# Unit 1's gate half by seven block products; four sums of h on GpSimd; three transfers made earlier

## The chip, the cores and the metric

The kernel runs on one core of a Trainium2 chip. The core has TensorE (PE; its weight loads are shown apart as PEld), VectorE (DVE), ScalarE (ACT), GpSimd (POOL) and SyncE (SP), each with an instruction queue of its own that it works through in order. Transfers are issued from the queues of SP and POOL. The metric is the device time of one execution in microseconds (us); lower is better.

## The reference

One layer of an encoder on 512 tokens with a model width of 2048, in float32. What matters here:

```python
h = rms_norm(x, pre_mix_g[l])
z = h @ w_in[l]                                  # q, k, v and u
a = chunked_attention(q, k, v, rel_bias[l])      # 8 heads of 128
p = multiscale_pool(u, pool_w[l], pool_scale[l])
m = jnp.concatenate([a, p], axis=-1) @ w_o[l]
x = x + rms_norm(m, post_mix_g[l])
h = rms_norm(x, pre_ffn_g[l])
up = causal_dwconv(h @ w_up[l], conv_w[l], conv_b[l])
y = (jax.nn.gelu(up[..., :D_FF], approximate=True) * up[..., D_FF:]) @ w_down[l]
x = x + rms_norm(y, post_ffn_g[l])
```

D_FF is 5632. The product h @ w_up has 2 x 5632 columns.

## The kernel before

**Numbers.** Every float32 operand is split into a rounded high part and a rest (`split`, lines 138 to 146: ScalarE rounds at L140, VectorE subtracts at L141). A plain product takes three matmuls of 512 columns for each block of 128 x 128 weights (`mm3`, L162, L164, L165). Products by the seven block products of Strassen's scheme take their block factors from sums of quarters of the weights and of h; `mm2` (L170 and L176) does each with one matmul of 512 and one of 256 columns for a block of weights.

**Stages.** The tokens' half products with w_in come first: q and k, then v (`v_steps`), then the other heads of q and k by seven blocks, then the heads' attention and u. Then come the products with w_o (`wo_product`), the norm, and h, turned and split, in four tiles gT0 to gT3 (`hT`). Then w_up: 5632 columns are 22 units of 256, and each unit has a gate half (p = 0) and an up half (p = 1). The first PLAIN = 3 halves (unit 0's two, unit 1's gate half) are plain products. The rest, 41 halves, are done by seven blocks (`Factors`, `seven`, `keep`, `keep_all`). Last come the products with w_down.

**Around the change.** Unit 0's halves go to four PSUM banks, `ups`, of the eight that the pool has. `h_sums(i)` for i = 0, 1 makes the sums of h's quarters that the seven blocks need: h5, h6 and h3 (tiles `hs`), each half (i) in turn. `whole` adds high part and rest of a quarter into one tile of 128x1024 (L1301), four times for each i; subtractions follow (L1309, L1312, L1314, L1317), and splits into `hs`. `h_difference` then overwrites one quarter of h by a difference. `up(1, 0, ...)` is unit 1's plain gate half; between its quarters it calls `spread2`, which turns the norm's factor into rows on TensorE (L223), and copies them out of PSUM as R on VectorE (L1267), and the gate and product of unit 0, which read `ups` and so free its banks.

The blocks of the series are named (k, i): half k, product i of 1, 6, 7, 4 (bank qa), 5, 3 (qg) and 2 (qd). The order is written out: it begins (0,1), (0,2), (0,5), (1,1), (0,3), then goes on by a table of places. Products 1, 7, 2 and 4 read quarters of h itself; 5, 3 and 6 read h5, h3 and h6. Each block's weights, a raw tile of 128x1024, are split ahead (four blocks ahead, `AHEAD`) into one of four pairs of tiles; between two uses GpSimd's queue adds another quarter of w_up to the raw tile by an accumulating transfer (L1365). The raw tiles come over SP's queue (L1348).

**Transfers of sums.** `sums_in_dram` builds sums of blocks of w_o (`wt`) and of w_down (`t`) in device memory, by copies and accumulating transfers; `more_sums(n)` makes the next n of them. While `paced` is set, each is issued from GpSimd's queue behind a small memset that waits for the VectorE split last issued. Afterwards copies go over SP's queue. `ready_blocks` splits three blocks of w_down among the w_o products and writes them back.

**Order.** TensorE's instructions stand as the program writes them. The order on the other engines is set by the framework's scheduler when the program is built, and is fixed in the built program.

Of the kernel before, what the change touches and what calls it, by code (L numbers as in the profile page):

```python
# [27 lines left out]
EPS = 1e-6  # L28
WARM = 9
NU = KF // 2  # L30
PLAIN = 3
CU = 4
AHEAD = 3
SCALE = 1.0 / math.sqrt(DH)
# [47 lines left out]
def encoder_layer(ctx: ExitStack, tc: tile.TileContext, x, xT, vecs, rel, post_mix, post_ffn,  # L82
# [23 lines left out]
    def bank(name):  # L106
        return psum.tile([P, 512], F32, tag="ps", name=name)
# [221 lines left out]
    def more_sums(n):  # L329
        for _ in range(n):  # L330
            next(sums_step, None)
# [166 lines left out]
    psv = [bank(f"v0_{t}") for t in range(NT)]  # L498
    sums_of_x = x_sums()
    for n, _ in enumerate(v_steps(0, psv)):  # L500
        if n in (1, 3, 5, 7, 9, 11, 13):
            more_sums(1)
        for _ in range(2):
            next(sums_of_x, None)
        if n == 9:
            for i, v in enumerate(differences):
                split(*(hT[i][:, :, at, :] for at in AT[1]), v)
            early_x.close()
            p0 = mixing_w.enter_context(tc.tile_pool(name="p0", bufs=1, reuse_waits="tile"))
# [103 lines left out]
    with tc.tile_pool(name="p1", bufs=2, reuse_waits="tile") as p1:  # L613
# [156 lines left out]
        for h in range(3):  # L770
            if not h:
                run(2)
                ready_head(0)
            run(1)
            scores(h)
            if h:
                more_sums(1)
            run(1)
            if h:
                values(h - 1)  # L780
                more_sums(1)
            run(1)
            ready_head(h + 1)
            run(1)
            turn(h)
            if not h:
                v_ready()
# [3 lines left out]
        def mid(h):  # L791
            def step():
                values(h)
                more_sums(2 if h in (3, 4) else 1)
                if h == 2:
                    scores(3)
                elif h + 2 < HEADS:
                    ready_head(h + 2)
                if h == 3:
                    v_load(1)  # L800
            return step
# [37 lines left out]
        def ready_blocks():  # L839
            for at, j in ready_parts:  # L840
                v, hi = (p2.tile([P, 1024], dt, tag=tag, name=tag) for tag, dt in (("rw", F32), ("rwh", F32R)))
                lo = v.bitcast(F32R)
                nc.sync.dma_start(v.rearrange("p (a b) -> p a b", a=2),
                                  first_block(at[0], at[1] - 1, 0)[:, 2 * j:2 * j + 2, :])
                for _ in range(4):
                    yield
                split(hi, lo, v)
                yield
                for dest, part_ in zip(ready_w[at], (hi, lo)):
                    nc.sync.dma_start(dest[:, 2 * j:2 * j + 2, :], f32(part_).rearrange("p (a b) -> p a b", a=2))  # L850
                for _ in range(2):
                    yield

        ready_steps = ready_blocks()

        def wo_product(i, cc, left, between=None):
            ps = [bank(f"m{i}{cc}{t}") for t in range(2)]
            if cc and i in (2, 5, 6, 3):
                more_sums(1)
            for q in range(4):  # L860
                w = weights.get(f"wo{i}_{cc}_{q}")
# [343 lines left out]
    with tc.tile_pool(name="p3", bufs=2, reuse_waits="tile") as p3:  # L1205
# [40 lines left out]
                nc.vector.tensor_mul(z[:, j, :], ps[j], R)  # L1246
            return z

        def up(u, p, between=()):
            ps = [bank(f"up{u}_{p}_{j}") for j in range(2)]  # L1250
            between = list(between)
            for i in range(4):
                w = weights.get(f"w{p}{u}_{i}")
                factors.prefetch(4 - len(weights.specs) + weights.used)
                for kb in range(4 * i, 4 * i + 4):
                    for j in range(2):
                        mm3(ps[j], part(w, j, slice(kb % 4 * P, (kb % 4 + 1) * P)), g_both(hT, kb),
                            kb == 0, kb == KD - 1)
                step = between.pop(0) if between else None
                if step:  # L1260
                    step()
            return ps

        def spread2():
            psr = bank("R2")
            spread(psr, rt)
# [30 lines left out]
        def h_sums(i):  # L1297
            def whole(k, t):
                v = raw_x(f"q{k}{t}").rearrange("p (a b) -> p a b", a=4)
                hi, lo = quarter(k, t, i)  # L1300
                nc.vector.tensor_add(v, f32(hi), f32(lo))  # L1301
                return v

            def keep(n, v):
# [20 lines left out]
        class Factors:  # L1325
# [20 lines left out]
            def load(self, k, i):  # L1346
# [2 lines left out]
                    self.raw[k, what] = tile_  # L1349

                if i == 1 and (k, "w") not in self.raw:
                    raw("w" if k in self.alone else "x", raw4("wx") if k == self.alone[0] else raw_x("wx"), 0, 0)
                elif i == 5 and k == self.alone[0]:
                    raw("x", raw4("wx"), 0, 0)
                    self.add(k, "x", 1, 0)
# [55 lines left out]
        def keep(k, i):  # L1411
# [10 lines left out]
            elif i == 6:  # L1422
                zs[k, "m"] = pair_tile("zm", 2)
                v = wide(zs[k, "m"][:, :1])
                keep.six = nc.scalar.activation(v, banks[k, "a"], AF.Copy).ins  # L1425
                nc.vector.tensor_add(v, banks.pop((k, "g")), v)
            elif i == 7:
                v = wide(zs[k, "m"][:, 1:])
# [26 lines left out]
        def first_left():  # L1455
# [4 lines left out]
            split(hi, lo, v)  # L1460
            return hi, lo

        for i in range(2):
            h_sums(i)
        z = up(1, 0, [spread2, lambda: product(0, gate(0, normed(ups[0])), normed(ups[1]))])
        z = normed(z)
        rights, firsts = [right(0, cc) for cc in range(2)], []
        for r in rights:
            next(r)
# [8 lines left out]
        for k, i in factors.order:  # L1478
            seven(k, i)
            keep(k, i)  # L1480
            if (k, i) == factors.order[0]:
                with ExitStack() as behind:
                    for ins in factors.third:
                        behind.enter_context(tc.issue_after(ins))
                    h_difference()
            if (k, i) == (0, 6):
                with tc.issue_after(keep.six):
                    gates[1] = gate(1, z)
            if (k, i) == (end, 6):
                summed.close()  # L1490
                pr = ctx.enter_context(tc.tile_pool(name="pr", bufs=2, side="right", reuse_waits="tile"))
# [256 lines left out]
```

## Time and profile before

| | us |
|---|---|
| three runs, median (lowest, highest) | 1858.98 (1856.39, 1862.3) |
| the profiled execution's own time | 1859.2 |
| its span, first to last instruction | 1857.4 |
| granted TensorE clock | 0.999 |
| PE busy, of the span | 1843.6 |
| DVE busy | 1540.8 |
| ACT busy | 1082.3 |
| POOL busy | 303.2 |

How to read what follows. A row of a timeline gives the start in us, the length in us, engine, line, operation, output tile <- input tiles, shape, how many instructions the row merges, and in brackets how long the engine was idle before it and what ended that. A matmul's length is that of one, and they overlap, so the start of the next counts. Rows of stretches give the stretch, its length, then busy time and number of instructions on PE, PEld, DVE, ACT and POOL, the granted clock, the busy share of the DMA engines, and GB/s. Rows of waits give who waited, for whom, the total, the number and the longest.

### The profile page before, as it was taken

The page shows a single profiled execution, that of the slowest core. Times are in us where ns is not written, and L with a number is a line of the kernel's source. Part 1 is how long each engine was busy: PE and PEld are TensorE (multiplying, and loading weights), DVE is VectorE, ACT ScalarE, POOL GpSimd, SP SyncE. Part 2 cuts the span into 40 slices and gives each one's busy share as a digit, 9 for nine tenths or more (in the row PEclk, how much of TensorE's full clock was granted, in tenths as well). Part 3 has the DMA queues.
Part 4 walks back from the last instruction along what each step waited for, and adds up shares of the span by engine and source line. Part 5 has one row for each costly group of instructions (what it writes and reads, how often), then busy time and mean ns, then how long its engine had stood idle before and what let it go on. Part 6 is the DMA issues. An engine that isn't in the chain of part 4 may idle for free.

```text
span 1857.4 us, 25457 instructions
## 1 busy us (share of the span) xinstructions
PE 1843.6 (99%) x9598; PEld 1584.8 (85%) x9598; DVE 1540.8 (83%) x1804; ACT 1082.3 (58%) x1376; POOL 303.2 (16%) x402
## 2 busy tenths in 40 slices
PE   9999999999999999999999999999999999999998
PEld 7888888888878888888888888888888888888886
DVE  6988777887698988888888888888887899899876
ACT  7654455456464666566666665656655655565553
POOL 3411000100000122212222122121121001111101
PEclk9999999999999999999999999999999999999999
DMA  8599978999994798988888888899888967777785
GB/s 319 174 318 297 320 232 236 267 255 331 348 328 144 186 213 195 208 210 195 203 198 206 209 199 198 204 206 202 200 176 293 363 220 175 193 210 178 176 229 159
DMA packets 139338, 426.01 MB, mean 229 GB/s; under 512 B 11920, under 2 KB 15376, under 8 KB 133520
## 3 DMA queue, kind: packets, MB, share of 16 engines
q0 software_dynamic: 54864, 173.56, 46.1%
q1 hardware_dynamic: 84352, 250.84, 38.4%
q8 instruction: 75, 1.23, 0.3%
q14 instruction: 47, 0.39, 0.1%
HBM read 370.35 MB, written 104.33 MB: 256 GB/s over the span
## 4 chain that ended last, share of the span: by engine, by line
PE 93%; DMA 3%; DVE 2%; ACT 1%; issue 1%; SPq 0%; DVEq 0%; POOL 0%; POOLq 0%; ACTq 0%
PE qa L170 18%; PE qa L176 10%; PE qg L170 9%; PE qg L176 5%; PE qd L170 4%; PE pa L164 4%; PE pa L165 4%; PE pa L162 4%; PE qd L176 2%; PE pg L164 2%; PE pg L165 2%; PE pg L162 2%; PE m L164 2%; PE m L165 2%; PE m L162 2%; PE v L164 2%
## 5 line engine op out<-in xcount | busy, mean ns | idle before, releaser
L140 ACT ACTIVATE wfh<-wx 128x1024 fp32r<-128x1024 f32 x192 | 203.4, 1059 | 152.7 <-PE qg L170 55.4
L170 PE MATMUL qa<-gT,wfh 128*128 128x512 f32 x1152 | 288.6, 392 | 0.0
L141 DVE TENSOR_TENSOR wfl<-wx,wfh 128x1024 fp32r<-128x1024 f32 x192 | 234.7, 1222 | 59.8 <-ACT wfh L140 44.8
L170 PEld LDWEIGHTS qa<-gT,wfh 128*128 128x128 f32 x1152 | 207.2, 189 | 37.1
L1365 POOL DMA_DIRECT2D wx<-in_w_up x122 | 104.7, 858 | 502.2 <-DVE wfl L141 473.8
L140 ACT ACTIVATE wfh<-wy 128x1024 fp32r<-128x1024 f32 x96 | 101.7, 1060 | 109.3 <-PE qg L170 57.9
L170 PE MATMUL qg<-h,wfh 128*128 128x512 f32 x656 | 162.2, 389 | 0.9 <-ACT zb L1421 0.9
L176 PE MATMUL qa<-gT,wfl 128*128 128x256 f32 x1152 | 161.2, 283 | 0.1
L176 PEld LDWEIGHTS qa<-gT,wfl 128*128 128x128 f32 x1152 | 151.6, 191 | 4.3 <-ACT zm L1425 0.3
L170 PEld LDWEIGHTS qg<-h,wfh 128*128 128x128 f32 x656 | 122.9, 188 | 26.7 <-ACT zb L1421 1.3
L141 DVE TENSOR_TENSOR bl<-b,bh 128x2048 fp32r<-128x2048 f32 x56 | 127.2, 2287 | 19.1 <-ACT bh L140 11.7
L140 ACT ACTIVATE bh<-b 128x2048 fp32r<-128x2048 f32 x56 | 106.1, 1913 | 55.1 <-DVE b L1129 22.8
L141 DVE TENSOR_TENSOR wfl<-wy,wfh 128x1024 fp32r<-128x1024 f32 x96 | 117.2, 1221 | 10.9 <-ACT wfh L140 6.4
L162 PE MATMUL pa<-bh,ah 128*128 128x512 f32 x320 | 124.5, 389 | 0.0
L164 PE MATMUL pa<-bl,ah 128*128 128x512 f32 x320 | 124.5, 389 | 0.0
L165 PE MATMUL pa<-bh,al 128*128 128x512 f32 x320 | 124.5, 389 | 0.0
L141 DVE TENSOR_TENSOR wfl<-wz,wfh 128x1024 fp32r<-128x1024 f32 x48 | 58.7, 1224 | 54.1 <-PE qa L170 54.1
L176 PEld LDWEIGHTS qg<-h,wfl 128*128 128x128 f32 x656 | 89.5, 190 | 6.4
L170 PE MATMUL qd<-gT,wfh 128*128 128x512 f32 x384 | 94.9, 389 | 0.0
L176 PE MATMUL qg<-h,wfl 128*128 128x256 f32 x656 | 91.5, 282 | 0.0
L170 PEld LDWEIGHTS qd<-gT,wfh 128*128 128x128 f32 x384 | 72.0, 188 | 14.9
L170 PE MATMUL qa<-h,wfh 128*128 128x512 f32 x328 | 82.1, 392 | 0.0
(550 smaller groups left out, 4363.5 us busy)
## 6 DMA issues: line engine op xcount, KB each, us to landing
wx<-in_w_up POOLq DMA_DIRECT2D x122, 512.0 KB, 6.1
b<-in_w_down SPq DMA_DIRECT2D x32, 1024.0 KB, 6.8
wt<-in_w_o POOLq DMA_DIRECT2D x24, 1024.0 KB, 15.8
wx<-in_w_up SPq DMA_DIRECT2D x43, 512.0 KB, 5.5
wz<-in_w_up SPq DMA_DIRECT2D x41, 512.0 KB, 6.0
wy<-in_w_up SPq DMA_DIRECT2D x41, 512.0 KB, 4.6
wy<-in_w_up POOLq DMA_DIRECT2D x41, 512.0 KB, 6.9
sum<-part POOLq DMA_DIRECT2D x38, 512.0 KB, 6.8
```

What stands on the lines that cost most here:

```text
L140: rounded = nc.scalar.activation(hi, src, AF.Copy)
L141: rest = nc.vector.tensor_sub(lo, src, f32(hi))
L162: nc.tensor.matmul(ps, l[0], r[0], start=first, stop=False, skip_group_check=onto)
L164: nc.tensor.matmul(low, l[0], r[1], start=False, stop=False, skip_group_check=onto)
L165: nc.tensor.matmul(ps, l[1], r[0], start=False, stop=last, skip_group_check=onto)
L170: nc.tensor.matmul(ps, w[0][:, kb], pairs[kb][0], start=fresh and not kb, stop=last, skip_group_check=not fresh)
L176: nc.tensor.matmul(ps[:, sl], w[1][:, kb], pair[:, sl], start=False, stop=last, skip_group_check=not fresh)
L1365: nc.gpsimd.dma_start(self.raw[k, what], self.block(k, m, kh), accum_op=ALU.add)
```

## The change

PLAIN becomes 2: unit 1's gate half joins the series as its half k = 0, which now has 42 halves. `up` goes away. `factors.prefetch(4)` comes ahead of the sums of h; `spread2` comes behind block (0,1), and the gate and product of unit 0 behind (0,2). Of the eight additions in `whole` the four of i = 0 move to GpSimd. The half k = 1 takes its first raw tile from the five tiles of `raw4`. One transfer of sums more is made among v, one more in the first head and one more in a later step of the heads; three fewer are left among the w_o products. The waits in `ready_blocks` are cut another way at the same total. The gate of unit 1, which stood behind (0,6) with an order of its own, is made by `keep_all`.

```diff
-PLAIN = 3
+PLAIN = 2
...
-        if n in (1, 3, 5, 7, 9, 11, 13):
+        if n % 2:
             more_sums(1)
...
             scores(h)
-            if h:
-                more_sums(1)
+            more_sums(1)
...
-                more_sums(2 if h in (3, 4) else 1)
+                more_sums(2 if h in (3, 4, 5) else 1)
...
-                for _ in range(4):
+                for _ in range(5):
                     yield
                 split(hi, lo, v)
                 yield
                 for dest, part_ in zip(ready_w[at], (hi, lo)):
                     nc.sync.dma_start(dest[:, 2 * j:2 * j + 2, :], f32(part_).rearrange("p (a b) -> p a b", a=2))
-                for _ in range(2):
-                    yield
+                yield
...
-            if cc and i in (2, 5, 6, 3):
+            if cc and i == 5:
                 more_sums(1)
...
-        def up(u, p, between=()):
...
                 hi, lo = quarter(k, t, i)
-                nc.vector.tensor_add(v, f32(hi), f32(lo))
+                (nc.vector if i else nc.gpsimd).tensor_add(v, f32(hi), f32(lo))
...
-                    raw("w" if k in self.alone else "x", raw4("wx") if k == self.alone[0] else raw_x("wx"), 0, 0)
+                    raw("w" if k in self.alone else "x", raw4("wx") if k < 2 else raw_x("wx"), 0, 0)
...
-                keep.six = nc.scalar.activation(v, banks[k, "a"], AF.Copy).ins
+                nc.scalar.activation(v, banks[k, "a"], AF.Copy)
...
+        factors.prefetch(4)
         for i in range(2):
             h_sums(i)
-        z = up(1, 0, [spread2, lambda: product(0, gate(0, normed(ups[0])), normed(ups[1]))])
-        z = normed(z)
...
                     h_difference()
-            if (k, i) == (0, 6):
-                with tc.issue_after(keep.six):
-                    gates[1] = gate(1, z)
+                spread2()
+            if (k, i) == factors.order[1]:
+                product(0, gate(0, normed(ups[0])), normed(ups[1]))
```

The changed program's lines are numbered a little lower: the additions of `whole` are L1284, the subtractions L1292 to L1300, the copy of R is L1250, the accumulating transfer L1348.

**First place: where the sums of h begin.** On GpSimd, before, behind the norm's roots (`small`, `rt`):

```order
L967 TENSOR_TENSOR small<-small,mhalf 128x2 x2
L218 TENSOR_TENSOR rt<-rt,mhalf 128x4
L1365 DMA wx<-in_w_up 128x1024 x3
L1365 DMA wy<-in_w_up 128x1024
L1365 DMA wx<-in_w_up 128x1024
L1236 DMA gd_0_5687<-ca 128x2x256
```

and now (q are the quarters' sums of `whole`, gT the tiles of h):

```order
L965 TENSOR_TENSOR small<-small,mhalf 128x2 x2
L1348 DMA wx<-in_w_up 128x1024
L218 TENSOR_TENSOR rt<-rt,mhalf 128x4
L1284 TENSOR_TENSOR q_5732<-gT_5003 128x1024
L1284 TENSOR_TENSOR q_5734<-gT_5001 128x1024
L1284 TENSOR_TENSOR q_5739<-gT_5001 128x1024
L1284 TENSOR_TENSOR q_5745<-gT_5003 128x1024
L1348 DMA wx<-in_w_up 128x1024 x2
```

The four additions stand behind the root L218, and an accumulating transfer stands ahead of it. On VectorE, before:

```order
L1057 TENSOR_REDUCE small<-small 128x4
L217 TENSOR_SCALAR rt<-small 128x4
L1301 TENSOR_TENSOR q_5716<-gT_4996 128x1024
L1301 TENSOR_TENSOR q_5718<-gT_4994 128x1024
L1301 TENSOR_TENSOR q_5723<-gT_4994 128x1024
L141 TENSOR_TENSOR w_0l<-w_0r,w_0h 128x1024
L1309 TENSOR_TENSOR q_5716<-q_5716,q_5718 128x1024
```

and now:

```order
L1055 TENSOR_REDUCE small<-small 128x4
L217 TENSOR_SCALAR rt<-small 128x4
L1292 TENSOR_TENSOR q_5732<-q_5732,q_5734 128x1024
L141 TENSOR_TENSOR wfl<-wx,wfh 128x1024
L1295 TENSOR_TENSOR q_5734<-q_5739,q_5734 128x1024
L141 TENSOR_TENSOR h_5698<-q_5732,h_5698 128x4x256
L1297 SCALAR_TENSOR_TENSOR q_5739<-q_5732,q_5739 128x1024
```

VectorE's first instruction behind L217 now reads two tiles that GpSimd writes. From there to the copy of R stand 25 instructions of 128x1024, where 26 stood before.

**Second place: the fourth block of the series.** On TensorE, now, with the engines that each row waits for (qa_5775, qd_5812 and qg_5860 are the banks of half 0, qa_5885 that of half 1; wfh and wfl the weights' parts; h_5698 is h5):

```order
L223 MATMUL R_5798<-ident,rt 128x128 [waits PE_49,Pool_49]
L170 MATMUL qd_5812<-gT_5003,wfh 128x512 [waits Activation_49]
L176 MATMUL qd_5812<-gT_5003,wfl 128x256 [waits DVE_49]
L170 MATMUL qg_5860<-h_5698,wfh 128x512 [waits Activation_49]
L170 MATMUL qg_5860<-h_5698,wfh 128x512 [waits DVE_49]
L170 MATMUL qa_5885<-gT_5001,wfh 128x512 [waits DVE_49,Activation_49]
L176 MATMUL qa_5885<-gT_5001,wfl 128x256 x4
```

The rows between, which wait for nothing, are left out. The first matmul of qa_5885 reads no VectorE result, yet waits for VectorE; the ones that read wfl behind it wait for nothing more. On VectorE, before, around the copy of R:

```order
L141 TENSOR_TENSOR h_5715<-q_5741,h_5715 128x4x256
L1317 SCALAR_TENSOR_TENSOR q_5747<-q_5741,q_5747 128x1024
L1267 COPY RR<-R_5795 128x512
L1268 TENSOR_SCALAR RR<-RR 128x512
L141 TENSOR_TENSOR wfl<-wz,wfh 128x1024
L141 TENSOR_TENSOR h_5714<-q_5747,h_5714 128x4x256
L1246 TENSOR_TENSOR z<-up_0_0_5256,RR 128x512
```

and now:

```order
L141 TENSOR_TENSOR h_5700<-q_5757,h_5700 128x4x256
L141 TENSOR_TENSOR gT_5002<-q_5752,gT_5002 128x4x256
L141 TENSOR_TENSOR h_5699<-q_5763,h_5699 128x4x256
L1250 COPY RR<-R_5798 128x512
L141 TENSOR_TENSOR wfl<-wx,wfh 128x1024
L1251 TENSOR_SCALAR RR<-RR 128x512
L1401 TENSOR_TENSOR za<-qd_5812,za 128x512
L1244 TENSOR_TENSOR z<-up_0_0_5265,RR 128x512
```

Before, one split of the sums of h stood behind the copy of R; now all of them stand ahead of it. The reads that free the banks of qd (L1401) and of unit 0's halves (L1244) follow it.

**Third place: GpSimd at the end of v** (wt are the sums of w_o's blocks, rt the first norm's factor), as the difference prints it:

```order
 L308 DMA wt_95<-in_w_o 128x4x512
+L296 MEMSET pace 128x1
+L308 DMA wt_95<-in_w_o 128x4x512
 L218 TENSOR_TENSOR rt<-rt,mhalf 128x4
 L296 MEMSET pace 128x1
-L308 DMA wt_95<-in_w_o 128x4x512
-L296 MEMSET pace 128x1
```

One accumulating transfer moves from behind the root to ahead of it.

More of the change, by code (lines that the diff above doesn't have):

```diff
@@ L1247, in normed @@
             return z
-        def up(u, p, between=()):
[L1250 to L1262, printed above, removed]
         def spread2():
```

## The prediction

> **What bounds the kernel now.** I read the page's first part and its chain, then TensorE's waits, then stretches of the span, and last the order of time on three engines around the place of the change.
>
> ```profile
> PE 1843.6 (99%) x9598; PEld 1584.8 (85%) x9598; DVE 1540.8 (83%) x1804; ACT 1082.3 (58%) x1376; POOL 303.2 (16%) x402
> PE 93%; DMA 3%; DVE 2%; ACT 1%; issue 1%; SPq 0%; DVEq 0%; POOL 0%; POOLq 0%; ACTq 0%
> ```
>
> TensorE is busy 1843.6 of 1857.4 us and makes 93% of the chain. So the kernel gains only by less matmul work or by fewer of the waits that are left, and these are all of them:
>
> ```profile
> PE up L162 <- DVE gT L144: 1.6, 1, 1.6
> PE idle L133 <- DVE mhalf L129: 1.1, 1, 1.1
> PE qg L170 <- ACT zb L1421: 0.9, 1, 0.9
> PE up L164 <- DVE gT L144: 0.7, 2, 0.5
> PE q L164 <- DVE gT L144: 0.6, 2, 0.3
> PE m L164 <- DVE wo_1l L141: 0.3, 1, 0.3
> PE m L164 <- DVE wo_0l L141: 0.3, 1, 0.3
> ```
>
> Columns: total, times, longest. They sum to 5.5 us, and none lies in v or the heads; the products with w_o wait 0.6 us. By stretches (length, then busy PE, PEld, DVE, ACT, POOL):
>
> ```profile
> 580.00:600.00 20.00, 20.00 (x90) 16.55 (x89) 17.98 (x19) 9.26 (x11) 2.87 (x2) 1.00 0.38 111
> 600.00:620.00 20.00, 20.00 (x92) 16.57 (x91) 19.64 (x21) 9.04 (x10) 0.00 (x0) 1.00 0.59 174
> 700.00:900.00 200.00, 200.00 (x1152) 176.68 (x1151) 166.38 (x197) 121.30 (x149) 44.45 (x53) 1.00 0.89 202
> ```
>
> At 600 to 620 us VectorE is 98% busy: it makes the sums of h there, under unit 1's plain gate half. In the steady series it is 83% busy. The plain half is thus the cover of a VectorE backlog, and the change removes this cover.
>
> **The matmuls: a gain of 2.4 us.**
>
> ```profile
> 601.50 0.39 PE L162 MATMUL up<-gT,w_0h 128*128 128x512 f32 x1
> 606.94 0.60 PE L223 MATMUL R<-ident,rt 128*128 128x128 f32 x4
> 607.29 0.48 PE L162 MATMUL up<-gT,w_1h 128*128 128x512 f32 x1
> 623.73 1.98 PE L170 MATMUL qa<-gT,wfh 128*128 128x512 f32 x8
> ...
> 713.31 1.84 PE qa L170 x8
> 732.81 1.84 PE qa L170 x8
> ```
>
> The plain half runs from 601.50 to 623.73; less the four turnings of R (607.29 - 606.94 = 0.35, which stay) that is 21.88 us. One half by seven blocks comes round every 732.81 - 713.31 = 19.50 us, or 2.786 a block. Gain 2.38. The three more splits and the recombining that the seven-block half needs on VectorE fall into the series, where the row at 700 us leaves a sixth of its time free.
>
> **The sums of h: a new wait of 14 us.** The series now starts at 601.5. Its third block, (0,5), reads h5; its fourth, (1,1), needs a PSUM bank. Four banks hold unit 0's halves, and R, qa, qd and qg fill the other four of eight, so qa of (1,1) takes the bank of R, and the printed order gives its first matmul a VectorE wait. R is copied out by VectorE only after all 25 instructions of the sums and the splits among them. So TensorE waits for that copy. Without a wait (1,1) would begin at 601.50 + 0.35 + 3 x 2.786 = 610.2.
>
> When is the copy done? Before, this stretch of VectorE is:
>
> ```profile
> 583.31 0.17 DVE L217 TENSOR_SCALAR rt<-small 128x4 f32<-128x4 f32 x1
> 583.39 3.49 DVE L1301 TENSOR_TENSOR q<-gT 128x1024 f32<-128x1024 f32 x3
> ...
> 613.17 0.68 DVE L1267 COPY RR<-R 128x512 f32<-128x512 f32 x1
> ```
>
> 26 instructions of 128x1024 without a gap in 613.17 - 583.39 = 29.78, so 1.145 each; 25 take 28.6, and the copy 0.7. Now VectorE's first instruction subtracts what GpSimd has added, all its other work stands behind that, and GpSimd's queue has the root (L218) in front of the adds:
>
> ```profile
> 583.56 1.91 POOL L218 TENSOR_TENSOR rt<-rt,mhalf 128x4 f32<-128x4 f32 x1 [23.07 <-DVE rt L217]
> ```
>
> The adds cannot start before 585.47, since the root needs VectorE's L217 at 583.3. No GpSimd add of 128x1024 is in this trace; the nearest are the 128x512 adds of the norm, with VectorE beside them:
>
> ```profile
> 39.25 2.68 POOL L408 TENSOR_TENSOR RR<-sq,RR 128x512 f32<-128x512 f32 x2
> 42.11 8.79 POOL L408 TENSOR_TENSOR RR<-sq,RR 128x512 f32<-128x512 f32 x4 [0.17 <-ACT sq L407]
> ...
> 43.25 2.01 DVE L423 TENSOR_TENSOR xT<-xT,xT 128x1024 f32<-128x1024 f32 x1 [0.23 <-ACT xT L409]
> 45.30 2.21 DVE L425 TENSOR_TENSOR xT<-xT 128x1024 f32<-128x1024 f32 x1
> 47.53 2.21 DVE L427 SCALAR_TENSOR_TENSOR xT<-xT,xT 128x1024 f32<-128x1024 f32 x1
> 49.66 2.31 DVE L141 TENSOR_TENSOR s<-xT,s 128x1024 fp32r<-128x1024 f32 x1
> ```
>
> With VectorE mostly idle an add takes 1.34, so 2.68 for twice the size (an estimate by size). Side by side both slow down: the adds to 8.79 / 4 = 2.20, VectorE's four to 8.74 together in place of 4.58. Four adds of 512 are two of 1024 and cost VectorE 4.2.
>
> So: two adds while VectorE stands still, 585.47 + 5.36 = 590.8. Then 28.6 + 0.7, and 4.2 for the third and fourth add, which run beside it: the copy ends at 624.3. TensorE waits 624.3 - 610.2 = 14.1. It falls in two pieces: h5 is the 16th instruction, done at 590.8 + 18.3 + 4.2 = 613.3, and (0,5) has by 608.4 done the four matmuls that need only its first half, so 4.9 there and 9.1 before (1,1). Behind the fourth block the splits are ahead again, since VectorE goes on while TensorE stands.
>
> Bounds: with no slowing beside each other the copy ends at 620.1 and the wait is 9.9; with adds at the slow rate even alone (4.40 each) it ends at 627.7 and the wait is 17.5. Were the adds free, 585.5 + 29.3 = 614.8 still leaves 4.6. I take 14.1, since the rows at 42 us have the same two engines and the same kinds of operands.
>
> [...]
>
> The accumulate that turns block (0,5)'s weights into a sum stands ahead of the root on GpSimd. Its raw tile takes the place that is now loaded at 575.52, so it is out of the way:
>
> ```profile
> 575.52 0.38 SPq L152 DMA_DIRECT2D w_2r<-in_w_up  x1
> ...
> wx<-in_w_up POOLq DMA_DIRECT2D x122, 512.0 KB, 6.1
> ```
>
> Landing takes 6.1 us, while VectorE needs 10 x 1.145 = 11.5 from (0,5)'s split to the second h6, whose rounding stands on ScalarE behind the next accumulate's landing. Hidden; a landing of 10 us would add 1.
>
> **The moved transfers: 0.1 us.** In v one accumulate more is issued ahead of the first root:
>
> ```profile
> 77.43 1.82 POOL L308 DMA_DIRECT2D wt<-in_w_o  x1
> 78.22 2.32 POOL L308 DMA_DIRECT2D wt<-in_w_o  x1
> 79.99 1.63 POOL L218 TENSOR_TENSOR rt<-rt,mhalf 128x4 f32<-128x4 f32 x1
> ...
> 82.33 0.60 PE L223 MATMUL R<-ident,rt 128*128 128x128 f32 x4
> ```
>
> Issues follow at 0.79; the root would end near 82.4 in place of 81.62, and TensorE wants it at 82.33: 0.1, at most 0.6, and nothing to gain. In the heads and at w_o TensorE waits for no transfer now; they can return 0.6 at most (the two rows on wo) and I cost them at nothing. The shifted splits of w_down's ready blocks likewise.
>
> **Sum**: 1859.2 - 2.4 + 14.1 + 0.1 = 1871.0. The profiled execution's 1859.2 lies 0.2 above the median of 1858.98, so I leave it.
>
> **Rivals.** (B) The engines don't slow each other: for it, the root at 583.56 stood beside three VectorE adds that took their usual 3.49; against it, the four rows at 43 to 52 us. Wait 9.9, time 1866.8. (C) The queue is slower: adds at 4.40 throughout, since their inputs are strided pieces of hT, and a landing of 10 us: wait 18.5, time 1875.4. Against it: the 1.34 add. (D) Not slower: the sums are made while unit 0's second half still runs, up to 601.50, so the copy ends before 610.2. It decides at one point: VectorE would have to enter its 25 instructions by 610.2 - 29.3 = 580.9. Against it L217 at 583.31, in front of them on its queue. Then only the matmuls count: 1856.9, within the noise. To be faster beyond noise the 2.3 us before 601 (rows on up) would have to go too, and more.
>
> **Chances**: forecast 0.58, B 0.15, C 0.13, D 0.14. Faster or slower means by over 0.3%, 5.6 us, about what a measurement of this kernel can tell. The first three are all slower: 0.86. D gives 0.10 same and 0.04 faster. Range 1863 to 1877: below it D, above it the upper bound with a late landing on top. The forecast's own range is 1867 to 1875.
>
> **What would show it.** Right: VectorE idle some 7 us before its first subtraction, released by GpSimd; GpSimd's four adds of 128x1024, two near 2.7 and two near 4.4, and VectorE at about 2.2 beside the latter; TensorE idle about 5 before qg and 9 before the second qa, released by h5 and by the copy of R; the series then without waits at 2.79 a block. Wrong: TensorE without a wait at the fourth block, the copy of R before 612, or waits in v, the heads or w_o of over 1 us.

## The result, and the profile after

| | before | after |
|---|---|---|
| median of four runs each (lowest, highest), us | 1858.74 (1856.39, 1862.3) | 1880.71 (1879.27, 1883.4) |
| ratio, 95% interval | | 1.0125 (1.0113 to 1.0137) |
| profiled execution, us | 1859.2 | 1881.4 |
| its span, us | 1857.4 | 1879.6 |

The change makes the kernel slower by 22.0 us. The forecast was 1871.0 with a range of 1863 to 1877: the direction was right, the size was not, and the range does not hold it. The profiled executions lie 22.2 apart, and that is the sum to account for.

The page of the changed kernel, busy time and chain of waits:

```profile
PE 1846.7 (98%) x9614; PEld 1586.5 (84%) x9614; DVE 1546.9 (82%) x1811; ACT 1088.3 (58%) x1384; POOL 317.2 (17%) x415
PE 81%; DMA 7%; DVE 6%; issue 3%; ACT 2%; POOL 1%; SPq 0%; DVEq 0%; POOLq 0%; ACTq 0%
```

TensorE's share of the chain fell from 93% to 81%, and DMA grew from 3% to 7%. The forecast spoke of VectorE and GpSimd only, so the DMA share is the first hint that something else happened.

**Where the time went** is read from landmarks: the first matmul of a kind, in both kernels. The rows are groups by tile; behind the durations stand the first and the last start. Kernel before:

```profile
L162 PE MATMUL m<-wo_0h,s x24: 388/389/397, 414.3 to 515.4; 128*128 128x512 f32 x24
L162 PE MATMUL pa<-bh,ah x320: 389/389/389, 1424.5 to 1804.7; 128*128 128x512 f32 x160
L162 PE MATMUL yl<-wb,gh x68: 277/389/389, 1805.3 to 1848.6; 128*128 128x512 f32 x60, 128*128 128x256 f32 x8
```

Changed kernel:

```profile
L162 PE MATMUL m<-wo_0h,s x24: 388/389/395, 418.3 to 520.4; 128*128 128x512 f32 x24
L162 PE MATMUL pa<-bh,ah x320: 389/389/389, 1444.4 to 1826.7; 128*128 128x512 f32 x160
L162 PE MATMUL yl<-wb,gh x68: 277/389/389, 1827.4 to 1870.7; 128*128 128x512 f32 x60, 128*128 128x256 f32 x8
```

The fourth landmark is the end of unit 0's halves: 601.50 before (the first plain matmul of unit 1), 607.87 now (the first block of the series, below).

| stretch | before | after | difference |
|---|---|---|---|
| start to w_o's first product with s (v, heads) | 414.3 | 418.3 | +4.0 |
| to the end of unit 0's halves | 187.2 | 189.6 | +2.4 |
| to the first product with w_down | 823.0 | 836.5 | +13.5 |
| to the last stage (yl) | 380.8 | 383.0 | +2.2 |

These are 22.1 us. Only the third stretch holds what the forecast was about. TensorE's waits in the changed kernel, the ones of 0.5 and more but for two at the start (total, times, longest):

```profile
PE qa L170 <- DVE RR L1250: 8.0, 1, 8.0
PE qg L170 <- DVE h L141: 3.7, 1, 3.7
PE u L162 <- DVE ptl L141: 2.4, 1, 2.4
PE up L162 <- DVE gT L144: 2.1, 1, 2.1
PE qa L176 <- ACT zm L1408: 1.5, 1, 1.5
PE pd L162 <- ACT ah L140: 1.1, 1, 1.1
PE m L164 <- DVE wo_0l L141: 0.7, 2, 0.5
PE s L164 <- DVE us L734: 0.7, 1, 0.7
PE R L223 <- POOL rt L218: 0.5, 1, 0.5
PE pd L165 <- DVE al L141: 0.5, 1, 0.5
```

The two forecast waits are there: qg for h5, and qa for the copy of R. The waits at u and at pd were not forecast, nor was that at qa for zm (it stands at 663.80, in the series). The wait at s comes and goes (0.9 in the runs `ready` and `h5_move` below, which keep the plain gate half), so it is not put down to the change.

**The seam.** The order of time on TensorE, changed kernel:

```profile
607.87 1.98 PE L170 MATMUL qa<-gT,wfh 128*128 128x512 f32 x8
609.69 1.11 PE L176 MATMUL qa<-gT,wfl 128*128 128x256 f32 x8
...
618.66 1.21 PE L170 MATMUL qg<-h,wfh 128*128 128x512 f32 x4 [3.70 <-DVE h L141]
619.69 1.88 PE L176 MATMUL qg<-h,wfl 128*128 128x256 f32 x8
629.57 3.75 PE L170 MATMUL qa<-gT,wfh 128*128 128x512 f32 x8 [7.99 <-DVE RR L1250]
...
634.18 2.00 PE L170 MATMUL qg<-h,wfh 128*128 128x512 f32 x8
```

From 607.87 to 634.18 are 26.3 us for the turnings of R and four blocks; unhindered they take 0.35 + 4 x 2.786 = 11.5. So 14.8 are lost. Of these 11.7 are the two waits. Most of the rest is speed: the fourth block takes 634.18 - 629.57 = 4.6 in place of 2.8, and the eight half-width matmuls at 619.69 took 1.88, where those at 609.69 took 1.11. These are 1.8 and 0.8 of the 3.1. The stretches say why (PEclk is the number behind POOL's):

```profile
620.00:640.00 20.00, 12.01 (x57) 10.27 (x57) 19.94 (x23) 12.20 (x14) 2.57 (x3) 0.67 0.86 228
640.00:660.00 20.00, 20.00 (x115) 17.50 (x114) 16.79 (x22) 11.65 (x16) 5.04 (x6) 1.00 0.90 215
```

The granted clock is 0.67 over 620 to 640 us, and 1.00 over 640 to 660; over the fourth block's first eight matmuls (629.57 to 633.12) it is 0.50, and right behind that block (634.18 to 637) 1.00. Behind the first wait it is 1.00 over the four matmuls from 618.66 to 619.69, and 0.50 from there to 622. So here part of the work behind each wait is done at half the clock; the 1.8 lost behind the wait of 8.0 and the 0.8 behind that of 3.7 lie there. The length of a wait alone does not settle this: a wait of 2.1 us at unit 0's start in this kernel is followed by a granted clock of 0.66 (558 to 563 us), and one of 3.3 us in `best_hd`, below, by 1.00 (610 to 630 us).

VectorE and GpSimd in the same place:

```profile
589.68 0.17 DVE L217 TENSOR_SCALAR rt<-small 128x4 f32<-128x4 f32 x1
595.74 3.41 DVE L1292 TENSOR_TENSOR q<-q,q 128x1024 f32<-128x1024 f32 x1 [5.89 <-POOL q L1284]
599.07 3.44 DVE L141 TENSOR_TENSOR wfl<-wx,wfh 128x1024 fp32r<-128x1024 f32 x1
602.43 1.21 DVE L1295 TENSOR_TENSOR q<-q,q 128x1024 f32<-128x1024 f32 x1
...
628.74 0.68 DVE L1250 COPY RR<-R 128x512 f32<-128x512 f32 x1
```

```profile
589.94 1.03 POOL L218 TENSOR_TENSOR rt<-rt,mhalf 128x4 f32<-128x4 f32 x1 [3.04 <-DVE rt L217]
590.96 10.47 POOL L1284 TENSOR_TENSOR q<-gT 128x1024 f32<-128x1024 f32 x4
```

The row merges four adds of unequal length. The third and the fourth one by one:

```profile
595.68 2.39 POOL L1284 TENSOR_TENSOR q<-gT 128x1024 f32<-128x1024 f32 x1
598.03 3.39 POOL L1284 TENSOR_TENSOR q<-gT 128x1024 f32<-128x1024 f32 x1
```

The first two also take 2.39 each; VectorE idles 5.89 until they are done. The third begins just ahead of VectorE's first instruction and keeps its 2.39, while that instruction takes 3.41 in place of 1.21, so it is held up by 2.2. The fourth begins while this instruction is still at work, and takes 1.0 longer. VectorE's second instruction begins beside the fourth add and takes 3.44. So in each of these three overlaps the instruction that begins second is the longer one, by 1.0 to 2.2 us.

**The heads.** The load of v's second half (vl) was issued at 303.76 before and at 304.02 now, and landed after 6.8 us before, 9.6 now. ScalarE scales it as it lands. Before:

```profile
310.56 2.56 ACT L143 ACTIVATE vh<-vl,rt 128x512 fp32r<-128x512 f32 x4 [4.43 <-DMA vl<-vd]
```

After, with the matmul at which it shows:

```profile
313.60 2.56 ACT L143 ACTIVATE vh<-vl,rt 128x512 fp32r<-128x512 f32 x4 [7.21 <-DMA vl<-vd]
```

```profile
317.76 0.50 PE L162 MATMUL u<-gT,u_0h 128*128 128x512 f32 x1 [2.40 <-DVE ptl L141]
```

The scaling is 3.0 later, VectorE's part of it stands ahead of the split into ptl on its queue, and u takes a PSUM bank that this split reads.

**The start of w_down.** The second left factor's split, before and after:

```profile
1430.79 1.06 ACT L140 ACTIVATE ah<-gc 128x1024 fp32r<-128x1024 f32 x1 [2.40 <-DMA gc<-gd]
```

```profile
1455.43 1.06 ACT L140 ACTIVATE ah<-gc 128x1024 fp32r<-128x1024 f32 x1 [7.22 <-PE pa L165]
```

Before, it waits for its load, and is done long before it is needed (pd begins 10.9 us behind pa). Now it waits for TensorE's last matmul of the first product pa. No data passes between the two. The reading is that the tile which it writes lies where the first left factor's rest lay, and that product reads it; `place`, below, tests this.

### The profile page after: what moved, and what is told of

The parts are those of the page before. It is cut to its first block, busy times and chain, and to the rows that moved or that the text cites. A ratio compares the mean times of both kernels' runs of the same rounds, so it can differ in the third digit from the quotient of the medians.

```text
span 1879.6 us, 25526 instructions
## 1 busy us (share of the span) xinstructions
PE 1846.7 (98%) x9614; PEld 1586.5 (84%) x9614; DVE 1546.9 (82%) x1811; ACT 1088.3 (58%) x1384; POOL 317.2 (17%) x415
## 4 chain that ended last, share of the span: by engine, by line
PE 81%; DMA 7%; DVE 6%; issue 3%; ACT 2%; POOL 1%; SPq 0%; DVEq 0%; POOLq 0%; ACTq 0%
PE qa L170 18%; PE qa L176 9%; PE qg L170 9%; PE qg L176 5%; PE qd L170 4%; PE pa L164 4%; PE pa L165 4%; PE pa L162 4%; PE qd L176 2%; PE pg L164 2%; PE pg L165 2%; PE pg L162 2%; DMA rw<-in_w_down 1%; DMA wx<-in_w_up 1%; PE pd L165 1%
## 5 line engine op out<-in xcount | busy, mean ns | idle before, releaser
L170 PE MATMUL qa<-gT,wfh 128*128 128x512 f32 x1176 | 296.3, 394 | 8.0 <-DVE RR L1250 8.0
L140 ACT ACTIVATE wfh<-wx 128x1024 fp32r<-128x1024 f32 x196 | 207.6, 1059 | 153.8 <-PE qg L170 60.3
L141 DVE TENSOR_TENSOR wfl<-wx,wfh 128x1024 fp32r<-128x1024 f32 x196 | 241.8, 1234 | 57.2 <-ACT wfh L140 41.9
L170 PEld LDWEIGHTS qa<-gT,wfh 128*128 128x128 f32 x1176 | 212.6, 190 | 46.4 <-issue 8.3
L1348 POOL DMA_DIRECT2D wx<-in_w_up x125 | 107.3, 858 | 521.6 <-DVE wfl L141 483.5
L170 PE MATMUL qg<-h,wfh 128*128 128x512 f32 x672 | 166.6, 390 | 4.1 <-DVE h L141 3.7
## 6 DMA issues: line engine op xcount, KB each, us to landing
wt<-in_w_o POOLq DMA_DIRECT2D x24, 1024.0 KB, 19.5
```

Of the source, the lines that this page charges most:

```text
L140: rounded = nc.scalar.activation(hi, src, AF.Copy)
L141: rest = nc.vector.tensor_sub(lo, src, f32(hi))
L170: nc.tensor.matmul(ps, w[0][:, kb], pairs[kb][0], start=fresh and not kb, stop=last, skip_group_check=not fresh)
L1348: nc.gpsimd.dma_start(self.raw[k, what], self.block(k, m, kh), accum_op=ALU.add)
```

## The experiments

**The two halves of the change apart.** `transfers` is the kernel before with

```diff
-        if n in (1, 3, 5, 7, 9, 11, 13):
+        if n % 2:
             more_sums(1)
...
             scores(h)
-            if h:
-                more_sums(1)
+            more_sums(1)
...
-                more_sums(2 if h in (3, 4) else 1)
+                more_sums(2 if h in (3, 4, 5) else 1)
...
-            if cc and i in (2, 5, 6, 3):
+            if cc and i == 5:
```

and the waits in `ready_blocks`; `products` is the changed kernel with these lines as before.

> The kernel before with the moved transfers alone: one accumulate more in v, one more in head 0, one more in the middle of head 5's step, three fewer among the products with w_o, and w_down's ready blocks split one step later. Theory A (the transfers cost something by themselves, because v's second half and z of a head are loaded late beside them): 1864 to 1865, with the 2.4 us wait of u for ptl and the 2.3 us lateness of zq back, and 0.5 at v's root. Theory B (the forecast's: the transfers are hidden, and the 5 us that the changed kernel lost ahead of unit 0 came with the rest of the change or by chance): 1859 to 1859.6.

> The changed kernel with all transfers where they were before: seven blocks for unit 1's gate half and four sums on GpSimd alone. Theory A: 1875, so the products and the sums cost 16 and the transfers the remaining 6; TensorE has no wait above 1 us ahead of 551 us, and waits about 3.7 and 8.0 us at qg and qa. Theory B: 1881, as the changed kernel. The forecast's sum has 1870.9 for it.

Measured: transfers 1865.05 (ratio 1.0033, 1.0019 to 1.0046), products 1876.69 (1.0090, 1.0064 to 1.0116); the kernel before beside them 1859.17. Theory A holds, though `products` came out 1.7 above the 1875 expected. The two ratios add up to 1.0123, the change's own 1.0125. In `transfers` u waits 2.6 for ptl and R 1.0 for the root; in `products` neither wait is there, qg and qa wait 3.7 and 7.2, and pd waits 1.1 and 0.5. So the heads' loss belongs to the transfers and w_down's start to the products. All kept profiles agree on the first: m begins at 413.7 to 417.1 in the four with the transfers as before (the kernel before, `products`, `best_hd`, `best_bg`), and at 418.3 to 422.0 in the seven with the change's transfers. In `products`, with the same two waits at pd, the slowest matmuls of pd take 0.63 us where 0.39 is usual, and pa to yl takes 384.6; in the changed kernel none of pd takes more than 0.50, and the granted clock stays at 1.00 there (1455 to 1460 us).

**GpSimd's share of the sums, none and double.** The changed line, in `vector_adds` and in `gpsimd_eight`:

```diff
-                (nc.vector if i else nc.gpsimd).tensor_add(v, f32(hi), f32(lo))
+                nc.vector.tensor_add(v, f32(hi), f32(lo))
...
-                (nc.vector if i else nc.gpsimd).tensor_add(v, f32(hi), f32(lo))
+                nc.gpsimd.tensor_add(v, f32(hi), f32(lo))
```

> The changed kernel with all eight sums of h on VectorE. Theory A (GpSimd's adds lengthen VectorE's chain: 5.9 us idle ahead of it and 2 x 2.2 us blocked, for 4 x 1.145 us saved): the copy of R ends 5.5 to 6 us sooner, TensorE's two waits at qg and qa fall from 11.7 to about 6, time 1875. Rival (it is VectorE's amount of work that sets the copy, and GpSimd relieves it): four instructions more on VectorE, copy 4.6 us later, time 1885.

> The changed kernel with all eight sums of h on GpSimd. Theory A (a GpSimd add of 128x1024 holds up the VectorE instruction beside it for its whole 2.62 us): four times 2.2 us blocked for 4 x 1.145 us saved, copy of R some 4 us later, time 1884 to 1886. Rival (both engines work side by side once VectorE has begun): VectorE's chain is 4.6 us shorter, time 1876.

Measured: vector_adds 1877.33 (1.0093, 1.0073 to 1.0114), gpsimd_eight 1888.50 (1.0153, 1.0129 to 1.0178). Both rivals fall, and the times lie 2.3 and 2.5 above the expected 1875 and 1886. (The 2.62 of the expectation is the mean of the four unequal adds.) The intervals touch that of the changed kernel, so what shows the effect is the stretch from the end of unit 0's halves to pa: 829.9 with no add on GpSimd, 836.5 with four, 840.5 with eight. VectorE with all eight adds, `vector_adds`:

```profile
593.42 0.17 DVE L217 TENSOR_SCALAR rt<-small 128x4 f32<-128x4 f32 x1
593.50 3.49 DVE L1284 TENSOR_TENSOR q<-gT 128x1024 f32<-128x1024 f32 x3
...
625.41 0.69 DVE L1250 COPY RR<-R 128x512 f32<-128x512 f32 x1
```

From L217 to the copy of R are 32.0 us there, 39.1 in the changed kernel (four adds on GpSimd), and 43.8 with all eight there. The waits of TensorE at qg and qa together are 5.3, 11.7 and 15.5. The vector kernel's profiled run came 3.7 us later to w_o's first product than the changed kernel's, through places that the edit doesn't touch, so its time shows less of the gain than its waits. `gpsimd_eight` shows the two engines in each other's way, GpSimd first, then VectorE:

```profile
604.45 3.45 POOL L1284 TENSOR_TENSOR q<-gT 128x1024 f32<-128x1024 f32 x1 [4.64 <-DVE q L1297]
610.20 5.61 POOL L1284 TENSOR_TENSOR q<-gT 128x1024 f32<-128x1024 f32 x2 [2.30 <-DVE h L141]
```

```profile
604.41 1.23 DVE L1300 SCALAR_TENSOR_TENSOR q<-q,q 128x1024 f32<-128x1024 f32 x1
605.56 3.43 DVE L141 TENSOR_TENSOR wfl<-wz,wfh 128x1024 fp32r<-128x1024 f32 x1
```

VectorE's instruction at 604.41 came first and keeps its usual length, and the add that begins beside it takes 3.45 in place of 2.39. The next VectorE instruction then takes 3.43. Here too the one that begins second is the longer.

**R copied earlier.** `early_R` is the changed kernel with

```diff
-        for i in range(2):
-            h_sums(i)
+        h_sums(0)
+        spread2()
+        h_sums(1)
...
-                spread2()
```

> The changed kernel with R spread and copied between the two halves of the sums of h in place of behind both. Theory A (two waits with two releasers: h5 for qg, then R's bank for the second qa; behind both stands the same queue on VectorE): the wait of 8.0 us at qa for the copy of R is gone, the one for h5 grows from 3.7 to about 6, and a new one of 3 to 4 us comes at the third sum's block; together 9 to 10 in place of 11.7, time about 1878. Rival B (the bank alone sets the end): the 8 us go and nothing takes their place, time 1873. Rival C (VectorE's queue alone sets it, the bank is only where it shows): the sum of the waits stays 11.7.

Measured: one time of 1880.58, span 1878.8 beside 1879.6 for the changed kernel. The waits at the seam:

```profile
PE qg L170 <- DVE h L141: 6.5, 2, 5.8
PE qa L176 <- DVE wfl L141: 0.2, 1, 0.2
```

The 8.0 us for R's bank are gone, and the wait for h5 grew from 3.7 to 5.8, as Theory A has it; the new wait at h3 is only 0.7. But then qg waits 2.7 for ScalarE's copy zb at 650 us, which the changed kernel does for 0.4. From the end of unit 0's halves to pa are 835.2 us in place of 836.5. So the bank was the releaser of the second wait and not what set its price: what is needed next is late too. For h5 that is VectorE's queue. The copy zb stands on ScalarE's queue behind a split that waits 2.77 for its weights' accumulating transfer, which GpSimd issued at 640.66 behind a split of VectorE's; how much of this wait is VectorE's lateness no run shows.

**The start of w_down.** `ring` and `place` try the overlap of tiles. The first takes two unused places from the ring of split tiles, the second changes the order in which w_down's tiles are laid out:

```diff
+            for _ in range(2):
+                w4("place")
             hi, lo = (w4(f"a{p}").rearrange("p (u n) -> p u n", u=CU) for p in "hl")
...
-        for r in (product_part, later["wh"], half_g, later["raw1"], raw2, later["wl"], slot_h, slot_l, scratch):
+        for r in (product_part, later["wh"], half_g, later["raw1"], raw2, later["wl"], scratch, slot_h, slot_l):
```

> The changed kernel, with two unused places taken from the ring of eight split tiles ahead of the split of w_down's first left factor. Theory (the plain half took eight tiles of that ring, seven blocks take fourteen, so the first left factor now lies six places on, in the memory that the second left split is written to, and this split waits for the first products to have read it): the split of gc starts when its load lands, as before, TensorE's waits at pd (1.1 and 0.5 us) vanish, and the stretch from the first pa to the first yl is 380.8 us as before in place of 383.0; all else unchanged. Rival (the load of gc or the transfers around it are later): 383.0, waits at pd unchanged.

> The changed kernel with the scratch tile laid out ahead of the ring of left splits in w_down's part, so that the second left split no longer lies in the memory of the first one's rest. (The two unused places of the run before had left the addresses as they were.) Theory: the split of gc starts with its load and not with the end of pa's first products, TensorE has no wait at pd (1.1 and 0.5 us), and from the first pa to the first yl there are 380.8 us in place of 383.0. Rival (the load is late): 383.0, waits at pd as they are.

Measured: in `ring` nothing changed at pd (1.1 and 0.5; 383.1 us from pa to yl). Unused places did not move the addresses, so this run said nothing on the theory (its one time is 1884.00). In `place` the split waits for its load again:

```profile
1456.97 1.06 ACT L140 ACTIVATE ah<-gc 128x1024 fp32r<-128x1024 f32 x1 [3.79 <-DMA gc<-gd]
```

TensorE has no wait at pd, and pa to yl is 380.8 us (1449.3 to 1830.1), as before the change. That is the whole 2.2. (Its one time, 1884.17, has other losses: 1.1 at q ahead of v, 1.6 at wo_0l.)

**What makes v's load late.** Four runs vary what GpSimd's queue has issued when the load starts at 304 us. `mid3` is the changed kernel with `2 if h in (4, 5, 6) else 1`, one transfer fewer in head 3's step; `no_beside` has none from 289 to 324 us:

```diff
-                more_sums(2 if h in (3, 4, 5) else 1)
+                more_sums(0 if h == 3 else 1 if h == 2 else 2)
...
-                more_sums(1)
+                more_sums(0 if j == 1 else 2 if j == 2 else 1)
```

`v_move` and `h5_move` are the kernel before with one of the three moves alone, the first of `transfers`' lines or the third, and `i in (2, 5, 6)` at w_o.

> The changed kernel with one paced transfer moved from the step of head 3, in which the second half of v is loaded, to that of head 6. Theory (the load of v, issued at 304 us, shares the DMA engines with a second accumulate there and lands after 9.6 us in place of 6.8): it lands within 7 us, and u waits for ptl less than 0.5 us in place of 2.4; the waits at w_o stay. Rival (the shift of every later transfer by two places, not the one beside the load): wait of about 2.4 as it is.

> The changed kernel with no paced transfer issued in the 15 us ahead of the load of v's second half: the two of head 3's step and the one after the second u are made in later steps. Theory (what is in flight beside that load decides; one accumulate and two copies behind it in the kernel before gave 6.8 us, a copy first gave 9.3 to 11.8): the load lands within 6.8 us and u does not wait for ptl. Rival (the load is late whatever is beside it, since the heads run on other transfers of the same queue): 9 us and a wait of 2 us as in the changed kernel.

> The kernel before with the one transfer moved into v, ahead of the first root, and the last one among the products with w_o left out for it. Theory: R waits 0.5 to 1.0 us for the root on GpSimd (the forecast had 0.1, at most 0.6), and nothing else: no wait of u for ptl, since at head 3 only one place has moved. Rival (any shift of the transfers delays v's load): a wait of 2 us of u for ptl here too.

> The kernel before with one transfer moved to the step of head 5 alone, and the last one among the products with w_o left out for it. Theory (v's load at 304 us is late by what is issued ahead of it, so only moves ahead of head 3 count): the load lands within 7 us as in the kernel before, u does not wait for ptl, time 1858 to 1860. Rival (every one of the moved transfers crowds the heads): u waits for ptl or s waits by 2 us and more.

| run | issued on GpSimd's queue, 302 to 304.2 us | landing of vl, us | u waits for ptl, us |
|---|---|---|---|
| before | accumulate (wt), copy (t), copy (t) | 6.8 | 0 |
| after | copy (t), accumulate (t) | 9.6 | 2.4 |
| mid3 | copy (t), accumulate (t) | 9.3 | 2.1 |
| v_move | copy (t), copy (t) | 11.8 | 4.6 |
| no_beside | none | 4.7 | 0 |
| h5_move | as before | 6.8 | 0 |

The queue of the kernel before and of `v_move`, by issue:

```profile
302.62 1.24 POOL L308 DMA_DIRECT2D wt<-in_w_o  x1
303.41 1.36 POOL L301 DMA_DIRECT2D t<-in_w_down  x1
304.12 1.44 POOL L301 DMA_DIRECT2D t<-in_w_down  x1
```

```profile
302.94 0.74 POOL L301 DMA_DIRECT2D t<-in_w_down  x1
303.65 0.83 POOL L301 DMA_DIRECT2D t<-in_w_down  x1
```

The load is issued at 303.4 to 304.8 us in these runs; in the kernel before, the second copy follows it by 0.36. In the kept profiles with the first order (six) it lands after 6.8 to 7.2, in the seven with the change's transfers after 9.3 to 10.0, so this is not chance.

Two expectations fell. `mid3` lacks the accumulate that the changed kernel issues at 310.19 and the load is as late, and `v_move` moves the sequence by one place only and it is later still. `no_beside` shows that the transfers beside the load are the cause, and `h5_move`, which changes nothing ahead of head 3, that the move there is free in its one run (1858.51, beside 1858.82). In the table a late load goes with copies at the head of the queue, and an accumulate ahead of the copies with an earlier one. No run varies this alone, and why it is so, none shows. The one times are 1883.37 for `mid3` and 1862.47 for `v_move`, the kernel before beside them 1860.39. In `v_move` R also waits 0.8 for the root, and of the 6.8 by which m begins later than in the kernel before, 3.5 are made up by the start of unit 0; what lets it catch up was not followed. `no_beside` also shows that the transfers' cost does not vanish by being put off: w_o's first product with s starts 3.3 earlier than in the changed kernel, but m then waits 4.5 in place of 1.6 and unit 0 starts 2.4 later (560.4 and 558.0); its one time is 1887.31.

**The ready blocks.** `ready` is the kernel before with the waits in `ready_blocks` alone as in the change (5 steps and 1 in place of 4 and 2).

> The kernel before with w_down's ready blocks alone split one step later and stored one step sooner; all paced transfers as before. Theory (this shift is what the products with w_o and unit 0 pay for): from the first m of 414 us to the first up 139.5 us in place of 137.6, waits of m for wo of 1.3 to 1.6 us in place of 0.6, time 2 us above before. Rival (the accumulates into w_down's sums, which the changed kernel has done by then, or their absence): 137.6 and 0.6 as before.

Measured: 1858.22, beside 1858.82; 136.3 us from m to up. The rival holds: by this one run the edit alone costs nothing.

**All causes taken away.** `best_hd` keeps seven blocks for unit 1's gate half and has the transfers as before, all sums on VectorE, R copied early, scratch laid out first, and the split of the difference later:

```diff
-            if (k, i) == factors.order[0]:
+            if (k, i) == factors.order[4]:
                 with ExitStack() as behind:
```

`best_bg` begins the series in another order on top of it:

```diff
-                begin = [(0, 1), (0, 2), (0, 5), (1, 1), (0, 3)]
+                begin = [(0, 1), (0, 2), (1, 1), (0, 5), (1, 2), (0, 3)]
```

> Seven blocks for unit 1's gate half with each cost taken away that has been found: transfers as before, all sums of h on VectorE, R copied between the halves of the sums, the split of the difference issued three blocks later, scratch laid out first. Theory: VectorE's queue from 583.4 reaches the second half of h3 at about 617, TensorE wants it at 613.9, so a wait of 3 us is left, the 2.4 of the matmuls are kept: 1859 to 1861. Rival (the backlog is only moved to the next need): waits of 6 us and more, 1864.

> The same with the blocks begun in another order: the three blocks that need no sum of h first, (1,2) ahead of (0,3). Theory: 2.8 us more of cover, so h3 is in time, but the fifth block needs a PSUM bank that VectorE frees at about 616.3 where TensorE wants it at 613.0: a wait of 3 us for the bank, 1859 to 1861. Rival (the bank is freed in time): no wait, 1857.

Measured: best_hd 1865.27 (ratio 1.0040, 1.0027 to 1.0052), best_bg 1870.28 (1.0064, 1.0045 to 1.0082); the kernel before 1858.66. TensorE's waits in the series of best_hd:

```profile
PE qg L170 <- DVE h L141: 3.3, 1, 3.3
PE qa L176 <- ACT zm L1410: 2.8, 2, 1.4
PE qg L170 <- ACT zb L1406: 1.4, 1, 1.4
```

The wait for h3 is the 3 us expected, but 4.2 more follow, which the theory did not have (1859 to 1861 expected). ScalarE's copies of finished chains come late: zb at 634.71 behind an instruction that waits 2.44 for VectorE, a zm at 647.49 behind a split that waits 3.26 for its weights. From unit 0's end to pa are 828.1 us against 823.0. The rival, that the backlog moves to the next need, fits. For `best_bg` both expectations fell (1859 to 1861, and 1857): qd waits 2.7 for the bank, as the theory had it, but the waits for zm come to 5.1, and the eight matmuls behind the 2.7 take 3.06 in place of 1.82; unit 0's end to pa is 831.8. No version was found that is faster than the kernel before; the gain of 2.4 is smaller than what is left of the seam.

## Why the prediction was right or wrong

**Right: what bounds, and the seam's mechanism.** The plain gate half was the cover of a VectorE backlog, and the change took it away. Both waits came with the releasers named, h5 and the copy of R, and by `vector_adds` GpSimd's adds make 6.4 of their 11.7 (5.3 are left without them). The chain from L217 to the end of the copy was forecast as 41.0 us and took 39.7 (589.68 to 629.42): an add was put at 2.68 and took 2.39, and the root took 1.03 in place of 1.91.

**Right for a partly wrong reason: 14.1 at the seam.** 14.8 were lost, but as 11.7 of waiting and 3.1 of slower work. The sum took TensorE to go on at 2.786 a block. What was lost of the 3.1 ahead of the second wait only shortened that wait; the 1.8 behind it came on top, and the chain, shorter by 1.3, made up for most of it. That the two cancel is luck.

**Nearly right: two engines beside each other.** The rows at 42 us gave 4.2 for two adds, with both engines slowed. Here VectorE paid 2 x 2.2 = 4.4, and the fourth add 1.0. So the sum for VectorE held, but not the even slowing of both: the add that began first kept its 2.39, and the one that began second was the longer (VectorE 3.41 and 3.44 in place of 1.21, the fourth add 3.39), in `gpsimd_eight` too (an add of 3.45, VectorE 3.43). Whether the rows at 42 us come about in the same way is not shown.

**Not shown wrong: the matmuls' 2.4.** From the fourth block's end to pa (634.18 to 1444.4) are 810.2; the same place before is 623.73 + 4 x 2.786 = 634.9, and to pa 789.6. That is 20.6 for one half more, in place of 19.5. So 1.1 came on top. The waits there are 1.9 (1.5 for zm, 0.4 for zb), where the kernel before had 0.9 for zb; that is 1.0 of it. The forecast had the series without waits.

**Wrong, the step that failed: "In the heads and at w_o TensorE waits for no transfer now; they can return 0.6 at most (the two rows on wo) and I cost them at nothing."** An absence of waits in the profile of before bounds what can be gained, and nothing else. The step gave no bound for a loss, though each move ahead shifts all later transfers against the loads beside them. The first two stretches cost 6.4, and `transfers` alone 5.9 by the medians, 6.1 by the ratio; 0.1 was forecast, 0.6 at most for v's root. What the loss is made of: the load of v's second half lands after 9.6 us in place of 6.8, and u waits 2.4 for ptl; R waits 0.5 for the root (1.0 in `transfers`, 0.8 in `v_move`, where 0.6 was the most allowed for); m waits 1.6 in place of 0.6 for w_o's weights. The text had named it as a sign of error: "waits in v, the heads or w_o of over 1 us".

**Missed: 2.2 at w_down's start.** The seven blocks' splits were counted as work on VectorE. That another number of tiles in a ring decides which tile the next stage overwrites was not looked at. `place` gives the 2.2 back.

The sum made good: 1871.0 + 6.3 for the transfers (the 0.7 at s among them) + 2.2 + 0.7 at the seam + 1.1 in the series = 1881.3, beside 1881.4 for the profiled execution. The stretches make up the span, so that this sum comes out proves nothing by itself; which cause a stretch belongs to rests on the runs. Of the 2.4 between w_o and unit 0's end, 1.0 are the waits of m and 0.5 the longer wait of up for gT (2.1); `transfers` has both (1.6 and 2.1), `ready` and `h5_move` alone have neither. The rest of it, and which of the moved transfers makes these waits, stay open.

## What to carry to other kernels

A stage in which an engine is 98% busy under another's work can be cover: to take it away cost the backlog here (14.8 us at the seam for 2.4 of matmuls), and neither another releaser nor another engine for part of the work removed it (in `best_hd` the stretch from unit 0's end to pa is still 5.1 us longer than before). A transfer for which nothing waits can still have a price when it is moved, since its move shifts the later ones against the loads that are waited for (here a landing after 9.6 us in place of 6.8, and a wait of 2.4); bound its loss by the slack of the nearest such load. A mean over merged instructions can hide that one of them was held up (2.62 for three of 2.39 and one of 3.39): look at them one by one. When a change alters how many tiles a ring hands out, look at what then lies under the next stage's tiles (2.2 us here).

## What the runs showed of the hardware

- In the changed kernel a GpSimd add of 128x1024 float32 took 2.39 us, beside VectorE too where it began first (595.68); in it and in `gpsimd_eight` a VectorE instruction of 128x1024 with two inputs that began beside an add took 3.34 to 3.44 in place of 1.21, and an add that began while VectorE's was at work took 3.21 to 3.45.
- Behind a wait of 8.0 us eight matmuls of 512 columns took 629.57 to 633.12, 3.55 us, where 1.82 is usual (607.87 to the next form at 609.69). The length of the wait does not decide alone: behind the 3.3 of `best_hd` nothing was lost, and the granted clock stayed at 1.00 (610 to 630), while behind 2.7 in `best_bg` eight took 3.06 (618.12 to 621.18; granted clock 0.93 over 610 to 620 and 0.90 over 620 to 630). The same wait of 2.1 at unit 0's start is followed by 0.66 in the changed kernel (558 to 563) and by 1.00 in `transfers` (540 to 580). What decides, no run shows.
- The same load of 1 MB, issued at the same place, landed after 4.7 to 11.8 us, with different transfers at the head of GpSimd's queue.
